# Moving the r, k and v projections of an RWKV-7 layer from its preparation into its loop over head pairs, and starting the network's first loads before a side calculation

## The chip, the cores and the metric

The kernel runs on one core of a Trainium2 chip. That core has TensorE (PE in the profile, with PEld for its weight loads), VectorE (DVE), ScalarE (ACT), GpSimd (POOL), and SyncE (SP), which here only issues DMAs. The metric is the time of one execution on the device in microseconds (us); lower is better.

## The reference

A network of four layers works on 512 tokens (256 of context, 256 noisy) of width 1024. The token mixer of layers 0 and 3 is a gated DeltaNet, of layer 1 an S5 state-space model, of layer 2 RWKV-7; a SwiGLU feed-forward follows each. Before each half a layer's input is normalised, scaled and shifted by numbers made from the conditioning vectors `c` and `c_ctx` ("modulation"). Layer 2, the one that is changed most, is cut here to what matters:

```python
dx = shifted - h
xr, xw, xk, xv, xa, xg = [h + dx * mu[j] for j in range(6)]
r = xr @ w_rkv[0]
k = xk @ w_rkv[1]
v = xv @ w_rkv[2]
g = jax.nn.sigmoid(xg @ g1) @ g2
kk = l2norm(heads(k * k_k))
for d in range(2):      # both directions
    logw = -jax.nn.softplus(-(w0[d] + jnp.tanh(xw @ w1[d]) @ w2[d])) - 0.5
    decay = jnp.exp(-jnp.exp(logw))
    a = jax.nn.sigmoid(a0[d] + (xa @ a1[d]) @ a2[d])
    k_d = k * (1.0 + (a - 1.0) * k_a)
...
def step(S, xs):        # one token, per head and direction, heads of 64
    sa = einsum('bhvk,bhk->bhv', S, kk_t)
    S = S * w_t - sa * (kk_t * a_t) + v_t * k_t
    return S, einsum('bhvk,bhk->bhv', S, r_t)
...
out = (groupnorm(y) * ln_w + ln_b + bonus) * g  @ w_out
```

## The kernel before

All activations lie with channels on the 128 partitions and the 512 tokens along the free axis, so a 1024-wide activation is eight tiles of 128x512. A dense product (`dense8`) is done in split precision: weights and activations are cut into a rounded half and its remainder (`whi`, `wlo`; `rhi`, `rlo`), ScalarE making the first and VectorE the second, and `mm3` issues three 512-column products (L135 to L137) for each 128x128 block of weights, 24 for an output tile. One such group of three is called a dense group below.

Instructions are issued to each engine in one fixed order, which a scheduler sets when the kernel is built. An instruction that waits holds up all that stand behind it in the order of its engine. For SP that order is also the order of nearly all DMAs.

**Outset.** `body` (L1719) first calls `net.s5_params()` (L674 to L738): a chain of small VectorE and ScalarE operations on the S5 parameters, which stores its outcome (`pk`) and loads it back (`s5pk`). Then it makes the modulation of layer 0 by `mods` (L169 to L183): 32 tiles `mraw` of 256 KB stream in and go through TensorE (L171). Then layer 0 begins with `norm`, which calls `rstd` (squares L194, sums L196, a product with ones L201), multiplies (L217), and splits for the first dense products.

**RWKV preparation** (`rwkv`, the part with the pool "rwa"). `mix(j)` makes one of the six mixed inputs: eight L1080 operations on VectorE, eight rounded halves on ScalarE (L158), eight remainders (L159), of which every second goes to GpSimd. `low` makes a low-rank input. `main` runs over the eight 128-channel tiles f, each a pair of heads: a dense product for r, k or v, copied and stored to HBM, and then one of the low-rank outputs (decay with its scan L1131, rate, gate), stored as well.

**Pair loop** (`RwkvCore`, the part with the pool "rwb"). For each pair: `load_in` reads k, r, the decays and rates back and forms exponentials and products; `gram` multiplies keys and queries chunk by chunk (64 tokens; L1527) into two masked tiles GK and GR; `invert` inverts the triangular 64x64 chunk matrices, whose 32-row diagonal blocks `fsub` inverts on VectorE alone, in 31 steps of two operations (L437, L439); `tokens` prepares what each chunk adds; `chain` walks over the 8 chunks in both directions at once (L1646 S to bank, L1656, L1662, L1668, L1670), each step needing the one before; `finish` normalises, gates and multiplies by the output weights into the residual X (dense groups with `yh`). While the chains of pair f run, `Lane` objects hand out the steps of other pairs' work between their steps, `n` steps spread over `over` chain steps, begun `lag` steps late: `finish` of f-1, `invert` and `tokens` of f+1, `load_in` and `gram` of f+2.

Of the kernel before, what the change touches and what calls it, by code (L numbers as in the profile page):

```python
# [12 lines left out]
F32 = mybir.dt.float32  # L13
# [6 lines left out]
P = 128  # L20
# [7 lines left out]
class Net:  # L28
    def __init__(self, tc, d, ctx):
# [11 lines left out]
        self.last_act = None  # L41
        cp = self.cp
# [163 lines left out]
    def norm(self, l, which, ts=slice(0, T), f32=None, f3=False):  # L206
# [7 lines left out]
        r = self.rstd(ts)  # L214
# [812 lines left out]
    def rwkv(self, l, nxt):  # L1027
# [4 lines left out]
        with ExitStack() as st:  # L1032
# [24 lines left out]
            rm = cn([P, T], "rmark")  # L1057
            G.memset(rm, 1.0)
            G.memset(rm[:, 0:T:64], 0.0)
            gneps = cn([P, 1], "gneps")  # L1060
            G.memset(gneps, 64e-5)
            par = self.fsub_marks(cpool)
            spill = lambda n: dp.tile([KD, P, T], F32, name=self.nm(n), tag=n)
            sp = {n: spill("rw_" + n) for n in ("r", "k", "v", "c0", "c1", "a0", "a1", "g")}

            with self.weights(), self.banks(w=4), tc.tile_pool(name="rwa", bufs=1, reuse_waits="tile") as ap:
                lora = [[ap.tile([P, T], F32R, name=self.nm("lo"), tag=f"lo{n}{x}") for x in range(2)]
# [7 lines left out]
                def mix(j):  # L1075
                    new = lambda n, k: ap.tile([P, T], F32R, name=self.nm(n), tag=f"{n}{k}", bufs=2)
                    hh = [], []
                    for k in range(KD):
                        t = self.tmp()
                        V.scalar_tensor_tensor(t, dx[k], mu(j, k), hf[k], op0=mul, op1=add)  # L1080
                        hh[0].append(new("rhi", k))
                        hh[1].append(new("rlo", k))
                        self.sub = G if k % 2 else V
                        self.split(t, hh[0][k], hh[1][k])
                    self.sub = V
# [24 lines left out]
                def main(n, hh, extra):  # L1110
                    self.hhi, self.hlo = hh
                    for f in range(KD):
                        ps = self.dense8(d["rwkv_rkv"]["rkv".index(n), f])
                        t, put = store(n, f)
                        A.copy(t, ps)
                        put()
# [35 lines left out]
                main("k", hk, ("rwkv_a2", rate))  # L1152
                low(2, hl)
                main("v", mix(3), ("rwkv_g2", gate))
# [4 lines left out]
            with self.weights(2), self.banks(c=2, o=1, w=2, g=1), \  # L1159
# [3 lines left out]
                for x in (core.load_in(0, st[0]), core.gram(0, st[0]), core.load_in(1, st[1]), core.invert(st[0]),  # L1163
                          core.tokens(0, st[0]), core.gram(1, st[1])):
# [3 lines left out]
                for f in range(KD):  # L1168
                    o = self.ps("o")
                    lanes = [Lane(late, 10, 28, 2)]  # L1170
                    if f < KD - 1:
                        n = st[f + 1]
                        lanes += [Lane(core.invert(n), 36, 34), Lane(core.tokens(f + 1, n), 11, 14)]
                    if f < KD - 2:
                        n = st[f + 2]
                        lanes += [Lane(core.load_in(f + 2, n), 6, 14), Lane(core.gram(f + 2, n), 13, 16, 16)]
# [273 lines left out]
class RwkvCore:  # L1450
# [15 lines left out]
    def load_in(self, f, out):  # L1466
# [5 lines left out]
        k, r = self.load("k", f), self.load("r", f, 1)  # L1472
        c, a = [[self.load(f"{n}{dr}", f) for dr in range(2)] for n in "ca"]
        out.update(r=r, a=a, kd=[], Pp=[], Pi=[])
# [11 lines left out]
        for dr in range(2):  # L1486
# [4 lines left out]
            G.tensor_tensor(kd, kd, k, op=mul)  # L1491
            G.tensor_tensor(a[dr], a[dr], kn, op=mul)
            for n, t in (("Pp", Pp), ("Pi", Pi), ("kd", kd)):
                out[n].append(t)
            yield

    def gram(self, f, out):
# [4 lines left out]
        D = new("fsD", [P, 16, 32], 2)  # L1502
# [5 lines left out]
        for dr in range(2):  # L1508
# [6 lines left out]
            G.tensor_tensor(q4(BK[:, :, 0:64]), n4(a), n4(Pi), op=mul)  # L1515
            V.tensor_tensor(q4(KR[:, :, 64:128]), n4(r), n4(Pp), op=mul)
            G.tensor_tensor(q4(BK[:, :, 64:128]), n4(kd), n4(Pi), op=mul)
# [4 lines left out]
            gk, gr = new("GK", [P, 2, 8, 64], 4), new("GR", [P, 2, 8, 64], 4)  # L1522
            for h in range(2):
                for c0 in (0, 4):
                    pg = net.ps("g").rearrange("p (c n) -> p c n", c=4)
                    for c in range(4):
                        mm(pg[:, c], BK[H[h], c0 + c, 64 * h:64 * h + 128], KR[H[h], c0 + c], start=True, stop=True)  # L1527
                    V.tensor_tensor(gk[:, h, c0:c0 + 4], pg[:, :, 0:64],
# [286 lines left out]
```

## Time and profile before

| | us |
|---|---|
| median of 3 runs (range) | 4115.85 (4113.26 to 4117.21) |
| the profiled execution's own time | 4122.03 |
| its span in the profile | 4120.3 |
| TensorE busy | 3692.1 (90%) |
| VectorE busy | 2596.9 (63%) |
| ScalarE busy | 1984.0 (48%) |
| GpSimd busy | 486.7 (12%) |
| HBM traffic by DMA | 432.71 MB, mean 105 GB/s |

The busy times are sums over the whole span, and the stages of the network have different limits, so they are only a first orientation. [...] The layer 2 mixer runs from about 1977 to 2857 us of the span.

### The profile page before, as it was taken

To read this page: it belongs to the slowest core of one execution; us is meant where nothing else is said; L and a number is where in the kernel's file an instruction comes from. 1 tells how busy PE (TensorE), PEld (TensorE's weight loads), DVE (VectorE), ACT (ScalarE), POOL (GpSimd) and SP (SyncE) were. 2 spreads that over 40 slices of the span, in tenths; PEclk is the share of its full clock that TensorE was granted. 3 is DMA by queue.
4 is the path that set the end of the run, shared out by engine and by line. 5 is a ranking of instruction groups with operands and counts; after the bars stand their busy time and mean duration, and the time that the engine had idled before them with its cause. 6 is when DMAs were issued, how large, how long until landed. Compare 5 with 4: busy or idle time off the path is not lost.

```text
span 4120.3 us, 75194 instructions
## 1 busy us (share of the span) xinstructions
PE 3692.1 (90%) x28906; PEld 2865.7 (70%) x28906; DVE 2596.9 (63%) x6045; ACT 1984.0 (48%) x4291; POOL 486.7 (12%) x625
## 2 busy tenths in 40 slices
PE   3889999989999798999795899997999978899899
PEld 1667777757777676777564666674777767787798
DVE  4777788767776743333874466665333487888665
ACT  4566677653333334232552333434322367778654
POOL 0000000012222200000212343430000000000000
PEclk8999999989999898999896566678999987999999
DMA  4312111135665623444342111001445311121155
GB/s 149 116 65 87 53 48 50 45 98 187 208 209 175 246 92 121 156 157 134 104 165 99 37 37 40 29 19 61 134 159 159 96 63 32 53 71 55 58 178 161
DMA packets 243624, 432.71 MB, mean 105 GB/s; under 512 B 27968, under 2 KB 53184, under 8 KB 240832
## 3 DMA queue, kind: packets, MB, share of 16 engines
q1 hardware_dynamic: 243264, 427.90, 32.0%
q8 instruction: 227, 3.72, 0.4%
q14 instruction: 133, 1.09, 0.1%
HBM read 383.49 MB, written 44.30 MB: 104 GB/s over the span
## 4 chain that ended last, share of the span: by engine, by line
PE 73%; DVE 12%; ACT 8%; DMA 3%; issue 2%; POOL 1%; SPq 0%; DVEq 0%; ACTq 0%; POOLq 0%
PE psd L135 10%; PE psd L136 10%; PE psd L137 9%; PE psw L135 7%; PE psw L136 7%; PE psw L137 7%; DMA mraw<-in_modw 2%; PE psm L171 2%; PE psg L1527 2%; PE psi L528 2%; PE pso L1670 1%; PE pso L1668 1%; PE psc L1381 1%; PE pso L1393 1%; DVE wlo L129 1%
## 5 line engine op out<-in xcount | busy, mean ns | idle before, releaser
L129 DVE TENSOR_TENSOR wlo<-wraw,whi 128x512 fp32r<-128x512 f32 (+1 forms) x906 | 622.6, 689 | 711.3 <-ACT whi L128 684.1
L128 ACT CAST whi<-wraw 128x512 fp32r<-128x512 f32 (+1 forms) x906 | 553.2, 613 | 1045.5 <-PE psd L136 591.8
L135 PE MATMUL psw<-hhi,whi 128*128 128x512 f32 (+1 forms) x1536 | 589.0, 383 | 26.7 <-ACT q L370 8.0
L137 PE MATMUL psw<-hhi,wlo 128*128 128x512 f32 (+1 forms) x1536 | 572.2, 373 | 0.1
L136 PE MATMUL psw<-hlo,whi 128*128 128x512 f32 (+1 forms) x1536 | 571.8, 372 | 0.4 <-DVE hlo L159 0.4
L135 PEld LDWEIGHTS psw<-hhi,whi 128*128 128x128 f32 x1536 | 296.4, 193 | 99.1 <-ACT whi L128 12.9
L137 PEld LDWEIGHTS psw<-hhi,wlo 128*128 128x128 f32 x1536 | 295.1, 192 | 51.6 <-issue 2.5
L136 PEld LDWEIGHTS psw<-hlo,whi 128*128 128x128 f32 x1536 | 296.3, 193 | 47.5 <-issue 3.1
L135 PE MATMUL psd<-hhi,whi 128*128 128x512 f32 (+1 forms) x784 | 296.0, 378 | 14.8 <-ACT hhi L158 14.8
L136 PE MATMUL psd<-hlo,whi 128*128 128x512 f32 (+1 forms) x784 | 289.6, 370 | 0.0
L137 PE MATMUL psd<-hhi,wlo 128*128 128x512 f32 (+1 forms) x784 | 288.9, 368 | 0.2 <-DVE wlo L129 0.2
L135 PE MATMUL psd<-fh,whi 128*128 128x512 f32 (+1 forms) x704 | 261.3, 371 | 0.0
L136 PE MATMUL psd<-fl,whi 128*128 128x512 f32 (+1 forms) x704 | 257.3, 366 | 0.0
L137 PE MATMUL psd<-fh,wlo 128*128 128x512 f32 (+1 forms) x704 | 256.8, 365 | 0.0
L237 DVE SCALAR_TENSOR_TENSOR X<-psd,modT,X 128x256 f32<-128x256 f32 x376 | 165.9, 479 | 110.3 <-PE psd L137 109.3
L171 PE MATMUL psm<-mraw,cs 128*32 128x256 f32 x1280 | 144.3, 416 | 68.5 <-DMA mraw<-in_modw 67.8
L135 PEld LDWEIGHTS psd<-hhi,whi 128*128 128x128 f32 x784 | 149.1, 190 | 62.6 <-ACT hhi L158 19.8
L136 PEld LDWEIGHTS psd<-hlo,whi 128*128 128x128 f32 x784 | 148.9, 190 | 28.0 <-DVE hlo L159 3.0
L137 PEld LDWEIGHTS psd<-hhi,wlo 128*128 128x128 f32 x784 | 149.2, 190 | 24.9 <-DVE wlo L129 0.6
L135 PEld LDWEIGHTS psd<-fh,whi 128*128 128x128 f32 x704 | 132.9, 189 | 34.5 <-ACT whi L128 11.1
L137 PEld LDWEIGHTS psd<-fh,wlo 128*128 128x128 f32 x704 | 133.0, 189 | 21.7
L136 PEld LDWEIGHTS psd<-fl,whi 128*128 128x128 f32 x704 | 133.0, 189 | 21.6 <-issue 1.6
(529 smaller groups left out, 7939.2 us busy)
## 6 DMA issues: line engine op xcount, KB each, us to landing
mraw<-in_modw SPq DMA_DIRECT2D x384, 256.0 KB, 3.3
wraw<-in_ffnin SPq DMA_DIRECT2D x352, 256.0 KB, 3.0
wraw<-in_gdn_qkvz SPq DMA_DIRECT2D x192, 256.0 KB, 2.7
wraw<-in_ffnout SPq DMA_DIRECT2D x160, 256.0 KB, 2.8
wraw<-in_gdn_out SPq DMA_DIRECT2D x64, 256.0 KB, 2.6
wraw<-in_rwkv_rkv SPq DMA_DIRECT2D x48, 256.0 KB, 3.0
s5ca<-ca SPq DMA_DIRECT2D x32, 256.0 KB, 3.1
s5in<-it SPq DMA_DIRECT2D x32, 256.0 KB, 4.2
```

Of the source, the lines that this page charges most:

```text
L128: nc.scalar.copy(hi[:, :n], raw[:, :n])
L129: self.sub.tensor_tensor(lo[:, :n], raw[:, :n], hi[:, :n].bitcast(F32), op=ALU.subtract)
L135: mm(out, whi, ahi, start=start, stop=False)
L136: mm(out, whi, alo, start=False, stop=False)
L137: mm(out, wlo, ahi, start=False, stop=stop)
L171: nc.tensor.matmul(ps[64 * x + 32 * q:64 * x + 32 * q + 32, :256], self.cs[:, k, :], w[:, q * 256:q * 256 + 256], start=(k == 0), stop=(k ...
L237: nc.vector.scalar_tensor_tensor(self.X[:, f, c], ps[:, c], self.modT[l][:, gate, f, s:s + 1], self.X[:, f, c], op0=ALU.mult, op1=ALU.add)
L528: mm(o, x, y, start=True, stop=True)
L1381: mm(p, Z[:, dr * 8 + v * 4 + c], x, start=True, stop=True)
L1393: mm(oc, w, at[hd][:, cs], start=first, stop=(step % 2 == 1 and hd == 3))
L1527: mm(pg[:, c], BK[H[h], c0 + c, 64 * h:64 * h + 128], KR[H[h], c0 + c], start=True, stop=True)
L1668: mm(o[H[h], cs], S[H[h]], KR[H[h], c, 64:128][:, rev], start=first[h], stop=False)
```

## The change

**Outset.** `body` begins the modulation first: seven steps of `mods`, then `net.rstd()`, whose result `norm` later takes from `net.early`, then `s5_params`, then the rest of `mods`.

**RWKV preparation.** `main` makes r, k and v only for the first two pairs; the halves of the three mixed inputs are stored to HBM instead (`rw_x`, 48 stores of 256 KB). All remainders are made on VectorE. `mix(3)` stands ahead of `low(2)`.

**Pair loop.** A new step `project` makes r, k and v of pair f+2 while pair f runs: for each of the three outputs, eight dense groups, each with its 512 KB of both halves (`vx`, three buffers) loaded anew, and weights in half tiles (`halves`), 144 such loads for six pairs. `load_in` of f+2 follows late in the same pair, and `gram` moves from f+2 to f+1. `gram` alternates the two heads and takes two banks of w at once; both its masks are now on VectorE, its copies on ScalarE. `invert` uses `sub16`, which inverts 16-row blocks in 14 steps of two VectorE operations and joins them with 128 small TensorE products (32x16). GpSimd's products and scalings go to VectorE and ScalarE. PSUM banks are shared out as c2, o1, w3 instead of c2, o1, w2, g1; the two banks `d` of dense products stay.

```diff
+        self.early = None
...
-        r = self.rstd(ts)
+        r = self.early or self.rstd(ts)
+        self.early = None
...
-                        self.sub = G if k % 2 else V
                         self.split(t, hh[0][k], hh[1][k])
-                    self.sub = V
...
                     self.hhi, self.hlo = hh
+                    j = "rkv".index(n)
+                    for k, parts in enumerate(zip(*hh)):
+                        for x in range(2):
+                            nc.sync.dma_start(sp["x"][j][k][:, x], parts[x].bitcast(F32))
                     for f in range(KD):
-                        ps = self.dense8(d["rwkv_rkv"]["rkv".index(n), f])
-                        t, put = store(n, f)
-                        A.copy(t, ps)
-                        put()
+                        if f < 2:
+                            ps = self.dense8(d["rwkv_rkv"][j, f])
+                            t, put = store(n, f)
+                            A.copy(t, ps)
+                            put()
...
-            with self.weights(2), self.banks(c=2, o=1, w=2, g=1), \
+            with self.weights(4), self.banks(c=2, o=1, w=3), \
...
-                for x in (core.load_in(0, st[0]), core.gram(0, st[0]), core.load_in(1, st[1]), core.invert(st[0]),
-                          core.tokens(0, st[0]), core.gram(1, st[1])):
+                for x in (core.fetch(0, st[0]), core.load_in(0, st[0]), core.gram(0, st[0]), core.invert(st[0]),
+                          core.tokens(0, st[0]), core.fetch(1, st[1]), core.load_in(1, st[1])):
...
-                    lanes = [Lane(late, 10, 28, 2)]
+                    lanes = [Lane(late, 12, 22, 2)]
                     if f < KD - 1:
                         n = st[f + 1]
-                        lanes += [Lane(core.invert(n), 36, 34), Lane(core.tokens(f + 1, n), 11, 14)]
+                        lanes += [Lane(core.gram(f + 1, n), 12, 12), Lane(core.invert(n), 22, 20, 13),
+                                  Lane(core.tokens(f + 1, n), 11, 16, 13)]
                     if f < KD - 2:
                         n = st[f + 2]
-                        lanes += [Lane(core.load_in(f + 2, n), 6, 14), Lane(core.gram(f + 2, n), 13, 16, 16)]
+                        lanes += [Lane(core.project(f + 2, n), 27, 31), Lane(core.load_in(f + 2, n), 6, 6, 28)]
...
+    def project(self, f, out):
+
+        net, nc, new = self.net, self.nc, self.new
+        for n in "krv":
+            j = "rkv".index(n)
+            ps = net.ps("d")
+            for k, w in enumerate(self.halves(net.d["rwkv_rkv"][j, f])):
+                x = new("vx", [P, 2, T], 3)
+                nc.sync.dma_start(x, self.sp["x"][j][k])
+                x = x.bitcast(F32R)
+                net.mm3(ps, *w, x[:, 0], x[:, 1], k == 0, k == KD - 1)
+                yield
+            t = out[n] = new("in_" + n)
+            nc.scalar.copy(t, ps)
             yield
...
+            for c0 in (0, 4):
+                pg = [net.ps("w").rearrange("p (c n) -> p c n", c=4) for _ in H]
+                for c in range(4):
+                    for h in range(2):
+                        mm(pg[h][:, c], BK[H[h], c0 + c, 64 * h:64 * h + 128], KR[H[h], c0 + c], start=True, stop=True)
...
-        TD = yield from net.fsub(self.gp, self.par, out["D"], lambda n: new(n, [P, 16, 32]))
+        TD, UD = yield from net.sub16(self.gp, self.par, D, lambda x, u: D[x, u],
...
-        w = net.wtile(net.d["rwkv_out"][f])
+        w = self.halves(net.d["rwkv_out"][f])
...
-                if 1 in layers:
-                    net.s5_params()
+                with tc.tile_pool(name="first", bufs=32, reuse_waits="tile") as fp, net.banks(m=2):
+                    first = net.mods(l, range(2 if l == 0 else 6), "m", net.raw_tile(fp, bufs=32))
+                    for _ in range(7):
+                        next(first)
+                    net.early = net.rstd()
+                    if 1 in layers:
+                        net.s5_params()
+                    for _ in first:
+                        pass
```

The first place is the order of DMAs on SP at the outset; `prm` and `s5pk` belong to `s5_params`, `mraw` to the modulation, `wraw` are weights of layer 0. Before:

```order
L71 DMA cc<-in_cc 128x16
L674 DMA prm_107<-in_s_prm 128x192
L738 DMA s5pk<-pk 128x2560
L169 DMA mraw_277<-in_modw 128x512
...
L169 DMA mraw_407<-in_modw 128x512
L1218 DMA cw_493<-in_gdn_conv 128x160
L1221 DMA gnw_496<-in_gdn_norm 128x1
L320 DMA dtb_595<-in_gdn_dtb 64x2
L127 DMA wraw_600<-in_gdn_ab 128x512
```

With the change:

```order
L72 DMA cc<-in_cc 128x16
L170 DMA mraw_105<-in_modw 128x512
...
L170 DMA mraw_157<-in_modw 128x512
L676 DMA prm_197<-in_s_prm 128x192
L170 DMA mraw_360<-in_modw 128x512
...
L170 DMA mraw_434<-in_modw 128x512
L128 DMA wraw_600<-in_gdn_ab 128x512
...
L128 DMA wraw_807<-in_gdn_qkvz 128x512
L740 DMA s5pk<-pk 128x2560
L128 DMA wraw_874<-in_gdn_qkvz 128x512
```

The modulation's loads now stand right behind the inputs, and `s5pk` has moved behind them and behind the first weights.

The second place is TensorE in the second half of a pair in the middle of the loop; L1646 and L1656 (L1692 and L1702 with the change) are the two products of the chain between which VectorE makes `x`. Before:

```order
L1646 MATMUL psc_21130<-S_24203,KR_22690 64x64 x2
L1668 MATMUL pso_23793<-KR_22690,S_24203 64x64
L1646 MATMUL psc_21131<-S_24247,KR_22814 64x64 x2
L1656 MATMUL psc_21130<-x_24241,U_23714 64x64 x2
L1656 MATMUL psc_21131<-x_24278,U_23714 64x64 x2
L1670 MATMUL pso_23793<-GR_22719,VS_23070 64x64
```

With the change (`vx` are streamed inputs of the projection, L507 is `sub16`):

```order
L1692 MATMUL psc_20475<-S_24480,KR_22914 64x64 x2
L1714 MATMUL pso_23905<-KR_22914,S_24480 64x64
L1692 MATMUL psc_20476<-S_24534,KR_23030 64x64 x2
L507 MATMUL psw_24706<-fsL_24223,fsUD_24614 32x16 x36
L1702 MATMUL psc_20475<-x_24528,U_23806 64x64 x2
L507 MATMUL psw_24706<-fsL_24223,fsUD_24614 32x16 x19
L136 MATMUL psd_24439<-vx_24771,whi_24470 128x512
L137 MATMUL psd_24439<-vx_24771,whi_24470 128x512
L138 MATMUL psd_24439<-vx_24771,wlo_24471 128x512
L136 MATMUL psd_24926<-vx_24933,whi_24928 128x512
L137 MATMUL psd_24926<-vx_24933,whi_24928 128x512
L138 MATMUL psd_24926<-vx_24933,wlo_24929 128x512
```

Between the steps of the chain now stand dense groups of the projection and the products of the new inverse.

The third place is TensorE at the end of a pair, where the Gram products (L1527, then L1575) stand. Before:

```order
L1527 MATMUL psg_24196<-KR_24166,BK_24167 128x128 x4
L1479 MATMUL psd_24628<-acc,bd_19087 128x512
L1702 MATMUL psd_24691<-t_24689,bdm_19088 128x512
L1527 MATMUL psg_24213<-KR_24166,BK_24167 128x128 x4
L1605 MATMUL psw_24451<-fsTD_24435,GK_23456 32x32 x16
```

With the change:

```order
L1716 MATMUL pso_23905<-GR_23056,VS_23435 64x64
L1742 MATMUL psd_24963<-t_24896,bdm_19088 128x512
L1575 MATMUL psw_24914<-KR_24900,BK_24901 128x128
L1575 MATMUL psw_24915<-KR_24900,BK_24901 128x128
L1575 MATMUL psw_24914<-KR_24900,BK_24901 128x128
L1575 MATMUL psw_24915<-KR_24900,BK_24901 128x128
...
L1575 MATMUL psw_24915<-KR_24900,BK_24901 128x128
L136 MATMUL psd_24926<-vx_25026,whi_24947 128x512
L137 MATMUL psd_24926<-vx_25026,whi_24947 128x512
L138 MATMUL psd_24926<-vx_25026,wlo_24948 128x512
L1702 MATMUL psc_20475<-XV_24413,U_24799 64x64
```

Runs of products into one bank became products that change bank and head at each instruction in the first half of the tokens, beside dense groups and the first step of the next pair's chain.

## Rows read from the trace of the kernel before

**Rows 1.** The page: granted TensorE clock in 40 slices of the span, tenths

```profile
PEclk8999999989999898999896566678999987999999
```

**Rows 2.** Windows: stretch; length; busy PE, PEld, DVE, ACT, POOL; clock; DMA share; GB/s

```profile
1977.00:2196.00 219.00, 182.05 (x769) 137.16 (x770) 156.59 (x252) 114.58 (x215) 43.24 (x28) 0.91 0.44 148
2196.00:2290.00 94.00, 36.48 (x287) 27.28 (x286) 46.17 (x106) 26.65 (x49) 32.25 (x32) 0.54 0.17 56
2290.00:2857.00 567.00, 529.24 (x4776) 383.46 (x4774) 348.68 (x1016) 206.59 (x560) 199.79 (x277) 0.70 0.11 32
```

**Rows 3.** SP timeline at the outset: start, duration, line, transfer, count

```profile
4.72 0.48 SPq L674 DMA_DIRECT2D prm<-in_s_prm  x1
32.38 0.33 SPq L738 DMA_DIRECT2D s5pk<-pk  x1
36.85 21.27 SPq L169 DMA_DIRECT2D mraw<-in_modw  x32
```

**Rows 4.** TensorE timeline at the outset, first dense product

```profile
79.70 0.79 PE L135 MATMUL psd<-hhi,whi 128*128 128x512 f32 x1 [4.78 <-ACT hhi L158]
```

**Rows 5.** VectorE groups, 1977 to 2196: count | busy us, mean ns | idle before

```profile
L1080 DVE SCALAR_TENSOR_TENSOR t<-dx,rprm,hf 128x512 f32<-128x512 f32 x48 | 46.4, 999 | 0.0
L129 DVE TENSOR_TENSOR wlo<-wraw,whi 128x512 fp32r<-128x512 f32 x54 | 39.8, 744 | 41.7 <-ACT whi L128 29.3 <-DMA wraw<-in_rwkv_rkv 2.8 <-DMA lw<-in_rwkv_g 2.0
L159 DVE TENSOR_TENSOR rlo<-t,rhi 128x512 fp32r<-128x512 f32 x24 | 22.8, 958 | 2.0 <-ACT rhi L158 2.0
```

**Rows 6.** A window of the RWKV preparation (columns as in the second group)

```profile
2040.00:2060.00 20.00, 20.00 (x92) 15.55 (x91) 19.00 (x30) 10.62 (x20) 0.00 (x0) 1.00 0.84 290
```

**Rows 7.** TensorE timeline between preparation and pair loop

```profile
2238.38 2.04 PE L1527 MATMUL psg<-KR,BK 64*128 64x128 f32 x8 [1.05 <-ACT GR L1530]
2241.34 2.07 PE L1527 MATMUL psg<-KR,BK 64*128 64x128 f32 x8 [0.92 <-ACT GR L1530]
...
2272.00 1.92 PE L1605 MATMUL psw<-fsTD,GK 32*32 32x32 f32 x64 [22.60 <-DVE fsTD L442]
```

**Rows 8.** VectorE group of the sub-block inverse in layer 0, 300 to 780

```profile
L483 DVE TENSOR_TENSOR fsL<-fsL,fsP 128x14 f32<-128x14 f32 (+6 forms) x70 | 13.8, 197 | 0.8
```

**Rows 9.** Windows inside the pair loop

```profile
2520.00:2541.00 21.00, 20.41 (x191) 15.59 (x185) 9.79 (x19) 7.53 (x19) 14.00 (x17) 0.54 0.11 33
2541.00:2562.00 21.00, 18.86 (x222) 13.90 (x221) 16.32 (x40) 8.59 (x23) 9.32 (x13) 0.98 0.26 76
```

**Rows 10.** A window inside the layer 0 loop

```profile
420.00:540.00 120.00, 111.66 (x1253) 90.06 (x1252) 94.38 (x231) 83.08 (x182) 3.05 (x6) 0.97 0.14 47
```

**Rows 11.** TensorE groups of 512-column products, layer 0 loop, 300 to 780

```profile
L135 PE MATMUL psw<-hhi,whi 128*128 128x512 f32 x243 | 101.5, 418 | 5.1 <-ACT t L370 2.9 <-ACT kT L370 2.1
L135 PE MATMUL psd<-Y,whi 128*128 128x512 f32 x95 | 41.3, 434 | 0.9 <-ACT whi L128 0.9
```

**Rows 12.** The TensorE group of the Gram products, pair loop

```profile
L1527 PE MATMUL psg<-KR,BK 64*128 64x128 f32 x434 | 92.2, 374 | 2.9 <-ACT GR L1530 2.3 <-DVE KR L1516 0.5
```

**Rows 13.** TensorE timeline at full clock, dense products among others

```profile
2548.20 0.51 PE L137 MATMUL psd<-yh,wlo 128*128 128x512 f32 x1
2548.55 0.39 PE L135 MATMUL psd<-yh,whi 128*128 128x512 f32 x1
...
2549.00 0.40 PE L137 MATMUL psd<-yh,wlo 128*128 128x512 f32 x1
2549.33 0.33 PE L1560 MATMUL psw<-ident,BK 64*128 64x64 f32 x2
```

**Rows 14.** TensorE timeline at full clock, Gram and chain products

```profile
2543.12 1.16 PE L1527 MATMUL psg<-KR,BK 64*128 64x128 f32 x8
2544.21 0.27 PE L1646 MATMUL psc<-S,KR 64*64 64x64 f32 x1
...
2827.36 0.33 PE L1646 MATMUL psc<-S,KR 64*64 64x64 f32 x4
2827.61 0.74 PE L1656 MATMUL psc<-x,U 64*64 64x64 f32 x8
```

## Prediction on record

> **What bounds the kernel now.** I read the granted clock by slices first, then windows by stage, then in each stage the timeline and the groups of the engine that the others wait for. The clock by slices shows one long dip [rows 1], and the windows place it: it is the RWKV mixer's second half. Three stretches matter [rows 2]. In the preparation (1977 to 2196, 219 us) TensorE is busy for 182 us and VectorE for 157, so both are nearly full. Between it and the first chain step (94 us) TensorE is busy for 36: there the stretch is a string of dependent steps. In the pair loop (567 us for eight pairs, 71 each) TensorE is busy for 529 at a mean clock of 0.70; VectorE has 349, ScalarE 207 and GpSimd 200, all far from full. The loop is bound by TensorE, and by TensorE running slow. Its clock is not even: 21 us at 0.54 stand right beside 21 us at 0.98 [rows 9]. The layer 0 loop holds 0.97 with TensorE busy for 112 of 120 us [rows 10].
>
> At the outset SP stands at `s5pk` until `s5_params` is through (32.38), and the 32 modulation tiles begin only when that has landed, at 36.85 [rows 3]; the first dense product starts at 79.70 [rows 4].
>
> The sum is made against the profiled execution's 4122.0 us; the median is 6.2 lower.
>
> **Outset.** The 32 loads took 21.3 us to issue [rows 3]; the first can now issue where `prm` did, at 4.7 [rows 3]. Estimate: 4.7 + 21.3, and about 6 more because the 2 MB of X are in flight at the same time (at the same 8.4 MB in 21.3 us), so they are in by 32. In the trace 79.7 - (36.85 + 21.27) = 21.6 us lay between the last issue and the first dense product, and squares, sums and the product with ones, some 10 us of it, now stand ahead. So the first dense product comes at 32 + 11 = 43, 37 earlier. The side calculation's VectorE operations now run among those of the norm; if these must wait for all of it the gain falls to some 30, and without the X term it is 43. I take **-38**.
>
> **Preparation.** It loses 18 x 24 = 432 dense products. At 0.23 us each [rows 13] that is 98 of TensorE's 182 us, which leaves 84. VectorE then sets the pace: of its 157 us it loses 36 `wlo` at 0.744 (27 us) and gains 24 remainders from GpSimd; with a partner on GpSimd L1080 takes 0.999 and `rlo` 0.958, where the same size took 0.744 in `wlo` [rows 5]. At 0.744 for all the sum is 157 - 27 + 18 - 12 - 5 = 131, at 0.958 for the new ones and nothing else it is 153. With VectorE full at 131 the stretch gains 88, at 153 filled to nine tenths 49. I take **-60**. The 48 new stores (12.6 MB) find room: the busiest window moved 290 GB/s [rows 6] where the stretch averages 148 [rows 2].
>
> **Between.** The Gram tiles of pair 0 follow each other every 2.96 us, each waiting for ScalarE to empty the one bank [rows 7]. Eight of them at the product's own 2.07 would save 7 us. The inverse made TensorE wait 22.6 us for `fsub` [rows 7]; 28 operations of 0.197 [rows 8] make 5.5 us, I put 15 to 16 for them with gaps, transposes and the two joins through TensorE, so 7 us less. GpSimd's part goes to a faster engine and pair 1's Gram leaves: 8 us in all. Against it 72 dense products of pair 2 are now queued here, ahead of the inverse's: 17 us at full clock, 33 at half, in 58 idle us. Their 24 loads of 512 KB need 43 us at 290 GB/s [rows 6], so they fit too, but not by much. From -35 (all hidden) to +10 (half of them exposed and the other savings halved); I take **-25**.
>
> **Loop.** Its work in microseconds of full clock is 567 x 0.70 = 397. To it come
> - 360 dense products (432 less the 72) at 0.23: +83;
> - what it costs to put them among other shapes. The last product ahead of a run starts 0.35 before the next one, and 0.33 pass after its last [rows 13], where inside the run it is 0.23: 0.1 at each end. For 120 groups in twos that is 60 x 0.2 = +12 (0 if hidden, 24 alone);
> - the 128 small products and their joins for 7 pairs: 64 of such a size took 1.92 us at the low clock [rows 7], so about 2 us a pair at full: +14;
> - the Gram products: 8 take 1.09 us, while 4 chain products that change heads take 0.25 [rows 14]. These are half as wide, so by the column nothing is gained to, at most, half of 434 x 0.136 = 59 us [rows 12]; the row of the same width is nearer: -10 of a possible -30.
>
> Sum 397 + 83 + 12 + 14 - 10 = 496. [...]
>
> The clock decides what becomes of 496. In the layer 0 loop 3 x 338 dense products stand in 480 us [rows 11], 0.23 x 1014 / 480 = 48% of the time, at 0.97 [rows 10]. Here it is 192 products (64 groups of `finish`), 8% of the time, at 0.70. With the change it would be 552 products in some 590 us, 22%. On the straight line between the two the clock is 0.79; since a group now stands in nearly every chain step, while before they came in one run per pair (the 0.98 window, with its weights' 76 GB/s [rows 9], is such a run), I take 0.84: 496 / 0.84 = 590, **+23**. Bounds: 0.97 gives 511 (-56), 0.70 gives 709 (+142).
>
> VectorE in the loop: 349 / 8 = 44 us a pair [rows 2], less some 12 for the inverse, plus 7 from GpSimd, 3 for masks, 5 for weights: 47 of some 74, hidden. If it were not, a pair could not fall under 47. ScalarE rises from 26 to some 36, hidden likewise.
>
> **Sum.** -38 - 60 - 25 + 23 = -100: 4022 for the profiled execution, **4016** by the median.
>
> **Rivals.**
> - *The clock rises to the layer 0 loop's level.* For it: the 0.98 window. Against it: only 22% dense. Loop 511, total 4016 - 79 = 3937.
> - *The clock does not rise.* For it: rows at 0.54 with TensorE busy for 20.4 of 21 us [rows 9], so busy time alone does not bring it. Loop 709, total 4016 + 119 = 4135, slower than before. It decides from a loop of about 690, a clock of 0.72. A pair would take 100 us and TensorE would be full throughout.
> - *The streamed inputs come late.* A group that waits for its `vx` holds up the chain's products behind it. With three buffers a load can be issued three groups ahead, some 9 us where groups stand one per chain step, but 4 to 5 where they stand in twos, as in the order; 512 KB at 290 GB/s are 1.8 us plus the landing. I expect no wait. If each of the 120 waits 0.5 us, it is +60: 4076; at 0.8 all gain is gone.
> - *The preparation does not follow VectorE* but the string ScalarE, VectorE, TensorE at each mixed input: half the gain, 4046.
> - *The one bank left to `wout`*, while a projection holds the other, makes 64 groups wait about 0.5 us for the residual on VectorE, with chain products behind them: +30 at most, in the same range.
>
> **Chances.** My forecast (clock 0.77 to 0.92, between 3970 and 4070, the two small rivals included): 0.52. Clock at 0.92 or above, under 3970: 0.22. Late inputs, or a clock of 0.72 to 0.77, 4070 to 4108: 0.09. Clock not rising, or late inputs above 0.8 us: 0.17, of which 0.04 lie within 0.2% of before. Two tenths of a per cent (8 us) is about what a measurement of this kernel can tell from no change. For 8 in 10 the range runs from 3935 to 4100. Faster 0.83, same 0.04, slower 0.13.
>
> **What would show it.** Outset: the first `mraw` issue at about 5 and the first dense product near 43. Preparation: VectorE nearly full, the stretch near 160. Between: about 70. Loop: a clock of 0.8 or more in its windows, TensorE busy for over nine tenths, pairs of 70 to 77 us for the first six, and the chain of waits still on TensorE. It is wrong if TensorE's idle time in the loop ends on `vx` loads, or if the clock stays near 0.7, or if VectorE ends the waits there.

## The result and the profile after

The changed kernel takes 4019.78 us, the median of 4 runs (4012.52 to 4024.64); the kernel before took 4116.53 beside it. The ratio is 0.9763, with a 95% interval of 0.9743 to 0.9782: 2.4% faster, 97 us, where the prediction on record had 100. The profiled execution took 4024.64 by its own time, 97 less than that of before (4122.03). Three disturbed executions, two of the kernel before (7565 and 5793) and one of run e5 (4557), are left out of the ratios.

On the page (first the busy sums, then the granted clock by slices, in tenths of the full, as in [rows 1]) the sum of TensorE's busy time is almost the same as before, and the long dip of the clock is shorter and shallower:

```profile
PE 3677.6 (91%) x30954; PEld 2827.6 (70%) x30954; DVE 2558.7 (64%) x5962; ACT 2039.2 (51%) x4421; POOL 225.8 (6%) x312
...
PEclk8999999989999898999787899868999888999899
```

The windows of the RWKV mixer after the change answer to [rows 2]: preparation, what lies between, pair loop (length, busy PE, PEld, DVE, ACT, POOL, clock, DMA share, GB/s):

```profile
1934.00:2076.00 142.00, 100.13 (x340) 62.54 (x338) 123.71 (x244) 87.49 (x165) 2.45 (x4) 0.79 0.64 224
2076.00:2149.00 73.00, 46.04 (x580) 32.82 (x580) 36.79 (x92) 29.59 (x54) 0.00 (x0) 0.64 0.62 210
2149.00:2755.00 606.00, 587.91 (x6958) 415.87 (x6956) 348.41 (x954) 288.31 (x738) 6.23 (x12) 0.85 0.44 145
```

The preparation went from 219 to 142 us, the part between from 94 to 73. The loop grew from 567 to 606, with a clock of 0.85 in the place of 0.70, and 145 GB/s in the place of 32.

At the outset, SP and the first dense product on TensorE, beside [rows 3, 4]:

```profile
4.46 11.25 SPq L170 DMA_DIRECT2D mraw<-in_modw  x14
...
50.92 0.33 SPq L740 DMA_DIRECT2D s5pk<-pk  x1
```

```profile
42.59 0.79 PE L136 MATMUL psd<-hhi,whi 128*128 128x512 f32 x1 [5.61 <-ACT hhi L159]
```

The modulation's first load issues at 4.46, `s5pk` waits until 50.92 behind all that is urgent, and the first dense product starts 37.1 us earlier than at 79.70.

The stages add up for the two profiled executions. In the table the stages run from one TensorE instruction to another: first dense product, the RWKV norm's product with ones, last low-rank product, first chain step, the feed-forward norm's product with ones (so the edges lie a few us beside those of the windows).

| stage | before | after | change |
|---|---|---|---|
| to the first dense product | 79.7 | 42.6 | -37.1 |
| to the RWKV norm | 1899.5 | 1894.2 | -5.3 |
| RWKV preparation | 217.2 | 139.0 | -78.2 |
| between | 93.9 | 73.5 | -20.4 |
| pair loop to the next norm | 570.4 | 609.7 | +39.3 |
| the rest | 1259.6 | 1263.9 | +4.3 |
| span | 4120.3 | 4022.9 | -97.4 |

The pair loop's two rows (columns as above), before and after:

```profile
2290.34:2860.69 570.35, 528.96 (x4773) 383.27 (x4771) 352.22 (x1022) 209.57 (x564) 199.79 (x277) 0.70 0.11 32
```

```profile
2149.31:2759.01 609.70, 587.99 (x6958) 415.90 (x6957) 352.27 (x961) 290.99 (x742) 6.23 (x12) 0.85 0.44 144
```

Below, length times granted clock is called the us of full clock that a stretch holds: 570.4 x 0.70 = 399 before, 609.7 x 0.85 = 518 after.

In the preparation VectorE's two large groups show why it shrank more than was said (count, busy, mean ns; compare [rows 5]): all 48 mixes now take 0.744 each and all 48 remainders 0.684.

```profile
L1083 DVE SCALAR_TENSOR_TENSOR t<-dx,rprm,hf 128x512 f32<-128x512 f32 x48 | 34.7, 744 | 0.0
L160 DVE TENSOR_TENSOR rlo<-t,rhi 128x512 fp32r<-128x512 f32 x48 | 31.8, 684 | 0.7 <-ACT rhi L159 0.7
```

In the part between, TensorE's waits (us in total, times, longest) show the streamed inputs, 7.0 us, but more for the string of small steps of `load_in`:

```profile
PE psd L1488 <- ACT acc L1485: 14.3, 2, 8.3
PE psd L136 <- DMA vx<-rw_x: 7.0, 8, 1.5
```

In the loop the inputs cost 1.9 us in all. TensorE is idle for 18 of the 606 us, and these are its longest waits:

```profile
PE psd L136 <- ACT yh L159: 4.7, 2, 4.4
PE pso L1716 <- ACT VS L1704: 3.1, 7, 1.4
PE psd L136 <- DVE X L239: 2.0, 4, 0.9
PE psd L136 <- DMA vx<-rw_x: 1.9, 4, 1.0
```

And the clock of the pairs: one in the middle of the loop, with a projection beside it, and the last two, which have none:

```profile
2387.75:2460.37 72.62, 71.92 (x961) 51.27 (x961) 47.81 (x132) 40.56 (x102) 1.04 (x2) 1.00 0.67 222
2618.42:2689.80 71.38, 68.26 (x872) 49.99 (x871) 33.26 (x102) 30.04 (x82) 0.00 (x0) 0.69 0.03 9
2689.80:2759.01 69.21, 55.13 (x352) 34.73 (x351) 32.59 (x79) 23.85 (x64) 0.00 (x0) 0.70 0.10 31
```

### The profile page after: what moved, and what is told of

It reads as the page before. It is cut to its first block, busy times and chain, and to the rows that moved or that the text cites. A ratio compares the mean times of both kernels' runs of the same rounds, so it can differ in the third digit from the quotient of the medians.

```text
span 4022.9 us, 79144 instructions
## 1 busy us (share of the span) xinstructions
PE 3677.6 (91%) x30954; PEld 2827.6 (70%) x30954; DVE 2558.7 (64%) x5962; ACT 2039.2 (51%) x4421; POOL 225.8 (6%) x312
## 4 chain that ended last, share of the span: by engine, by line
PE 75%; DVE 10%; ACT 9%; DMA 3%; issue 2%; SPq 0%; POOL 0%; DVEq 0%; ACTq 0%
PE psd L136 11%; PE psd L137 10%; PE psd L138 10%; PE psw L136 8%; PE psw L137 7%; PE psw L138 7%; PE psm L172 2%; DMA mraw<-in_modw 2%; PE psi L530 2%; PE pso L1716 1%; PE pso L1714 1%; PE psw L1575 1%; PE psc L1390 1%; PE pso L1402 1%; DMA vx<-rw_x 1%
## 5 line engine op out<-in xcount | busy, mean ns | idle before, releaser
L129 ACT CAST whi<-wraw 128x512 fp32r<-128x512 f32 x854 | 521.3, 613 | 975.9 <-PE psd L137 548.3
L130 DVE TENSOR_TENSOR wlo<-wraw,whi 128x512 fp32r<-128x512 f32 x854 | 582.9, 685 | 653.6 <-ACT whi L129 645.7
```

Source lines behind the costliest of these rows:

```text
L129: nc.scalar.copy(hi[:, :n], raw[:, :n])
L130: self.sub.tensor_tensor(lo[:, :n], raw[:, :n], hi[:, :n].bitcast(F32), op=ALU.subtract)
```

## Experiments

"Loop" and "preparation" below are the stages of the table, from each run's profile. The times are medians, with the ratio to the kernel before.

### The outset alone (e1_outset)

The kernel before with `early`, and `body` as in the diff ahead of the prediction.

> The kernel before with the outset's change alone. In the trace of the changed kernel the first dense product came 37 us earlier, and the stretch from there to the RWKV preparation was 6 us shorter. If both belong to the outset, this kernel takes 4116 - 43 = 4073 us; if only the first dense product does, 4079; if an earlier start is given back later (weights and modulation loads that now meet), 4090 or more.

Measured: 4104.84, ratio 0.9962 (0.9947 to 0.9977): 12 us faster, not 37 or more. The profile has the gain where it was expected: first dense product at 42.2, RWKV norm at 1938.2, 41 us ahead of before. Then it is lost in a loop whose code was not touched. Its windows (whole loop, then two neighbouring pairs):

```profile
2249.36:2856.70 607.34, 563.38 (x4772) 408.74 (x4770) 356.15 (x1022) 210.83 (x564) 200.23 (x277) 0.65 0.10 30
2411.84:2511.00 99.16, 92.40 (x677) 66.91 (x676) 55.73 (x154) 30.82 (x81) 34.55 (x46) 0.62 0.09 28
2511.00:2576.62 65.62, 62.60 (x589) 45.54 (x589) 43.24 (x127) 25.25 (x69) 24.59 (x33) 0.63 0.13 42
```

607 us at 0.65 against 570 at 0.70: in us of full clock 395 against 399, so the loop holds the same work and takes longer by its clock. This profiled execution, at 4121, is the slowest of the six that were timed (4097 to 4121), and its mean clock over the whole span is 0.899, where the one at 4097 has 0.907. Of the three expectations the third, a gain given back, holds by its number; but the place is the loop, at a lower clock, and not loads that meet. Instructions in the loop do stand in another order here, since the scheduler laid out the whole program anew. The order is the same in all six executions, so it does not make the 24 us between them; whether it makes the loss of the median is not shown.

### The RWKV part alone (e9_rwkv_part_alone) and useless products beside the outset (e10_idle_products_and_outset)

The first is the changed kernel with the old outset in `body` and `norm`. The second adds the outset to the kernel e6 below.

> The changed kernel with the outset of before: the change's second half alone. The outset alone gave 12 us where its first dense product came 37 us earlier and the RWKV preparation began 41 us earlier; the loop of that kernel took 607 us at a clock of 0.65 where that of before took 570 at 0.70. If the two halves of the change simply add up, this kernel takes 4020 + 12 = 4032. If the outset's 41 us are earned in full where the loop's clock does not fall (theory), it takes 4020 + 41 = 4061, with a loop near 606 as in the changed kernel.

> The kernel before with the 16 useless dense groups a pair and with the outset of the changed kernel. Theory (the outset alone lost its gain to the loop's clock, which dense products hold up): the loop stays near 588 at 0.83, and the whole is 4140 less 41: 4099. If the loss has another cause (loads that meet, a different order), 4140 less 12: 4128.

Measured: e9 4051.77, ratio 0.9851 (0.9828 to 0.9875). Beside a loop at 0.86 the outset is worth 4051.8 - 4019.8 = 32 us, nearer to its 41 than to the 12 it gave alone; the two halves alone give 12 and 64 us, together 97. e10: 4105.30, ratio 0.9973 (0.9957 to 0.9989), 34 us less than e6 without the outset, and the same as e1's 4104.84: beside the new outset the useless products cost nothing. Both lie between the two expectations and nearer to the theory's. The loops of the two profiled executions:

```profile
2181.60:2788.70 607.10, 584.04 (x6958) 414.60 (x6957) 353.07 (x961) 290.61 (x741) 6.21 (x12) 0.86 0.44 145
```

```profile
2247.50:2855.40 607.90, 580.50 (x5103) 411.39 (x5101) 346.96 (x1022) 209.77 (x564) 196.51 (x277) 0.80 0.10 30
```

So the new outset brings the first dense product 36 to 38 us earlier in each kernel (42.2 and 43.3 here, 79.7 and 78.8 without it), and less of that is given back where dense products stand in the loop: 34 and 32 us are left, against 12 in e1. Why the loop gives it back is not shown. e10's profiled run, at 4119.9, is the slowest of ten (4094 to 4120), with its loop at 0.80 instead of e6's 0.83: also there something is given back.

### All of r, k and v in the preparation (e2_all_in_preparation)

```diff
-                    for k, parts in enumerate(zip(*hh)):
-                        for x in range(2):
-                            nc.sync.dma_start(sp["x"][j][k][:, x], parts[x].bitcast(F32))
...
-                        if f < 2:
+                        if f < KD:
...
-                        lanes += [Lane(core.project(f + 2, n), 27, 31), Lane(core.load_in(f + 2, n), 6, 6, 28)]
+                        lanes += [Lane(core.fetch(f + 2, n), 1, 4), Lane(core.load_in(f + 2, n), 6, 6, 28)]
```

> The changed kernel, but with r, k and v of all pairs made in the preparation as before and fetched in the loop: no streamed inputs, no dense products of the projection between the chains. Theory (the projection's products raise the clock of the loop): the preparation grows by about 65 us, the loop loses 384 products of 0.23 us (88 at full clock, of 515), but its clock falls back from 0.85 to about 0.70, so it takes 427 / 0.70 = 610 and gains nothing; the whole is about 4085. Rival (the clock of 0.85 comes from the alternating Gram products and the new inverse): 427 / 0.85 = 502 in the loop, the whole 4020 + 65 - 104 = 3981.

Measured: 4044.39, ratio 0.9818 (0.9798 to 0.9838): 25 us slower than the changed kernel. Preparation and loop:

```profile
1933.90:2135.40 201.50, 179.03 (x770) 135.74 (x770) 143.98 (x268) 112.94 (x213) 2.08 (x4) 0.93 0.48 158
2202.90:2780.40 577.50, 550.14 (x6574) 402.34 (x6573) 330.85 (x929) 264.10 (x691) 6.21 (x12) 0.67 0.10 31
```

The preparation grows by 62.5 us, the part between falls by 6.0, and the loop falls by 32.2 only, from 609.7 to 577.5, though 384 dense products have left it: its clock is 0.67 again. In us of full clock that loop holds 577.5 x 0.67 = 387, the changed one 609.7 x 0.85 = 518. The move put 131 us of full clock into the loop for 32 us of time. The theory's clock came, but its 610 us and 4085 did not: it put the work that is left at 427 instead of 387. The rival (clock 0.85 without the projections, 3981) is out. This loop has 1800 products more than that of the kernel before (6574 against 4773), all of them small, and its clock is no higher (0.67 against 0.70): more instructions alone do not raise it.

### Useless products in the kernel before (e6_idle_products_before) and in the last pairs (e5_idle_products_last_pairs)

```diff
+    def fill(self, n):
+        net, nc, x = self.net, self.nc, self.fx
+        for _ in range(n):
+            ps = net.ps("d")
+            for i in range(3):
+                nc.tensor.matmul(ps, x[:, :P], x, start=i == 0, stop=i == 2)
+            yield
...
+                    lanes += [Lane(core.fill(16), 16, 31)]
```

In e5, on the changed kernel, it is `fill(12)` for the last two pairs, with `x` from one loaded `vx`.

> The kernel before with useless work added: 16 dense groups in every pair of the loop (384 products of 512 columns, about as many as the changed kernel's projections have there; nothing is streamed, results not used). Theory (dense products raise the clock): 397 us of full clock plus 88 and some 12 for the change of shapes, at about 0.85 as in the changed kernel: 585 instead of 567, the whole some 4130, with the loop's clock at 0.82 or more. Rival (the clock does not follow them): 497 / 0.70 = 710, the whole some 4255.

> The changed kernel with useless work added: in the last two pairs, which have no projection, 12 dense groups each (72 products of 512 columns in all, on data that is loaded once, results not used). In the changed kernel these pairs take 71 and 69 us at a clock of 0.69 and 0.70, where pairs with a projection have 0.82 to 1.00. Theory (dense products between the chain's steps raise the clock): their work of 49 us of full clock each becomes 57, at 0.85 to 0.95 that is 60 to 67 us a pair, so the kernel gets faster by 6 to 15 us although it does more: about 4010. Rival (the clock there has another cause): 16 us of work more at 0.70, +24: 4044.

Measured: e6 4139.74, ratio 1.0062 (1.0043 to 1.0081). 384 products, 88 us at full clock, cost 24 us. Of them 54 stand ahead of the loop's first chain step, where TensorE was idle for much of the time; 330 (76 us) stand in the loop:

```profile
2287.00:2875.00 588.00, 560.99 (x5102) 399.04 (x5101) 348.64 (x1022) 209.98 (x564) 195.83 (x277) 0.83 0.11 31
```

0.83 in the place of 0.70, 588 us, 18 more than before; the theory said 585 and at least 0.82, the rival 710. Nothing else of the change is in this kernel, so dense products raise the clock by themselves.

e5: its three executions take 4018 to 4025, ratio 0.9771 (0.9751 to 0.9791), the same as the changed kernel's 0.9763: between theory (4010) and rival (4044). The last two pairs:

```profile
2618.91:2688.72 69.81, 69.81 (x906) 50.90 (x904) 34.40 (x105) 28.59 (x79) 0.00 (x0) 0.84 0.03 9
2688.72:2757.57 68.85, 56.01 (x386) 35.45 (x386) 32.53 (x80) 24.61 (x65) 0.00 (x0) 0.85 0.09 31
```

Their clock is 0.84 and 0.85 where it was 0.69 and 0.70, and they take 69.8 and 68.9 us where they took 71.4 and 69.2. 16 us of added work were free, but did not pay as the theory had it (60 to 67 us a pair). TensorE waits for nothing in the first of the two (busy for 69.8 of 69.8), so the room that the clock gives is just used up.

### The Gram products head by head (e3_gram_head_by_head)

```diff
-                for c in range(4):
-                    for h in range(2):
+                for h in range(2):
+                    for c in range(4):
```

> The changed kernel with the Gram products of one head after those of the other, all else (two banks at once, masks, copies) the same. The rows of the changed kernel give 24 alternating products in 2.2 us, 0.091 each, where before they stood 0.136 apart: 0.045 x 448 = 20 us of full clock, at 0.85 some 24 us: 4044. By the value that the prediction took (10 at full clock) it is 4032. If weight loads were hidden already, 4020.

Measured: 4044.49, ratio 0.9807 (0.9782 to 0.9832), the 24 us that were expected; but the trace does not bear out the reason. In both kernels a run of 24 Gram products stands ahead of a dense group between preparation and loop, first in the changed kernel, then here:

```profile
2104.71 2.26 PE L1575 MATMUL psw<-KR,BK 64*128 64x128 f32 x24
2106.90 0.50 PE L136 MATMUL psd<-vx,whi 128*128 128x512 f32 x1
```

```profile
2102.69 2.42 PE L1575 MATMUL psw<-KR,BK 64*128 64x128 f32 x24
2105.04 0.51 PE L136 MATMUL psd<-vx,whi 128*128 128x512 f32 x1
```

2.19 us against 2.35: 0.091 and 0.098 a product. The second run began at a lower clock: the dense products just ahead of it start 0.42 to 0.43 us apart (2101.28, 2101.71, 2102.13), those behind it 0.23 to 0.34. So heads that alternate save at most 0.007 x 448 = 3 us of full clock, not 20; summed over the loop, from start to start at the granted clock, these products take 47 and 48 us. The 0.136 that I had read from [rows 14] came from a run of eight with the change of shape at its end in it (inside it they stand 0.112 apart, at its end 0.20), which the longer runs over two banks spread; what else makes these faster is not separated. So the 4044 was met by luck. What the loop lost lies mainly in one pair, at a low clock:

```profile
2147.60:2782.40 634.80, 607.74 (x6957) 433.26 (x6957) 353.66 (x961) 291.28 (x742) 6.22 (x12) 0.83 0.42 138
2457.48:2562.01 104.53, 102.50 (x985) 72.22 (x984) 52.23 (x141) 44.13 (x107) 1.09 (x3) 0.70 0.45 151
```

104.5 us at 0.70, the pairs on either side 74 to 76. Its five executions lie from 4020 to 4049, with a mean clock of 0.937 in the one and 0.925 in the other, so the loss comes in some and not in others, in one and the same order of instructions. What decides it stays open.

### Remainders back on GpSimd (e4_remainders_on_gpsimd)

```diff
+                        self.sub = G if k % 2 else V
                         self.split(t, hh[0][k], hh[1][k])
+                    self.sub = V
```

> The changed kernel with every second remainder of the mixed inputs back on GpSimd. Theory (VectorE sets the pace of the preparation, and is slowed while GpSimd works beside it): 24 remainders of 0.68 leave VectorE (-16 us), but 48 mixes go from 0.744 back to about 1.0 (+12) and the 24 others from 0.68 to 0.96 (+7): VectorE's sum is the same within 5 us, and the time with it, 4020 to 4027. Rival (VectorE is simply relieved): 4004.

Measured: 4038.63, ratio 0.9807 (0.9794 to 0.9821), 19 us slower: both expectations missed, in the direction of the theory. VectorE's groups in the preparation:

```profile
L1083 DVE SCALAR_TENSOR_TENSOR t<-dx,rprm,hf 128x512 f32<-128x512 f32 x48 | 44.7, 953 | 0.0
L160 DVE TENSOR_TENSOR rlo<-t,rhi 128x512 fp32r<-128x512 f32 x24 | 23.5, 983 | 1.4 <-ACT rhi L159 1.4
```

The mixes went from 0.744 to 0.953, the remainders that VectorE kept from 0.684 to 0.983, those of the weights from 0.685 to 0.917. Its scans (L1138, here L1140) did not slow: 1.217 and 1.211; in the kernel before, where they take 1.215, none of the 16 has a GpSimd operation beside it. VectorE does 24 operations less and is busy for 132.6 us instead of 121.4. The preparation takes 151.5 us instead of 139.0. The trace of the kernel before shows the same by operation: the 28 mixes that run with nothing on GpSimd beside them take 0.742 each, the 20 others 1.36; of the remainders, the 6 alone 0.682, the 18 others 1.05. What the two engines share is not shown.

### The old inverse in the loop (e8_fsub_in_the_loop)

`first` is set for pair 0 alone.

```diff
-        TD, UD = yield from net.sub16(self.gp, self.par, D, lambda x, u: D[x, u],
+        if not first:
+            TD = yield from net.fsub(self.gp, self.par, D, lambda n: new("fs", [P, 16, 32], 3))
+            UD = new("fs", [P, 16, 32], 3)
+            nc.vector.transpose(UD, TD)
+        else:
+            TD, UD = yield from net.sub16(self.gp, self.par, D, lambda x, u: D[x, u],
...
-                        lanes += [Lane(core.gram(f + 1, n), 12, 12), Lane(core.invert(n), 22, 20, 13),
+                        lanes += [Lane(core.gram(f + 1, n), 12, 12), Lane(core.invert(n), 36, 20, 13),
```

> The changed kernel with the old inverse for pairs 1 to 7, in the loop, and the new one only for pair 0, ahead of it. Theory (the loop is bound by TensorE, the new inverse's products are cost there): 256 small products a pair leave, 17 us of full clock in all, 20 at 0.85: 4000. Rival (VectorE, with 12 us a pair more, 62 steps that stand among the chain's, makes the chain wait): no gain, or 10 to 20 us more, with TensorE waiting for VectorE's x and S.

Measured: 4010.10, ratio 0.9750 (0.9724 to 0.9776). That is 10 us below the changed kernel, but the intervals overlap. The loop:

```profile
2150.10:2753.70 603.60, 563.19 (x5166) 398.43 (x5165) 402.66 (x1179) 282.12 (x725) 9.39 (x18) 0.84 0.43 145
```

It takes 603.6 us instead of 609.7, with VectorE busy for 403 instead of 352 and 603.6 x 0.84 = 507 us of full clock instead of 518, 11 less. Both expectations hold in part: TensorE is busy for 25 us less (563 instead of 588), as the theory had it, but idle for 40 instead of 22, as the rival had it. This profiled execution, at 4022, is the slowest of the four (3999 to 4022), so the 10 us of the medians are not all in these rows.

### Modulation in the last pairs (e7_modulation_last_pairs, e11_half_modulation_and_fsub)

```diff
+                mod = Lane(self.mods(l + 1, range(6), "d", lambda: core.new("vx", [P, 2, T], 3)[:, 0]), 48, 62)
...
-                        for x in lanes:
+                        for x in lanes + [mod] * (f >= KD - 2):
...
-            net.ffn(l, ts, l + 1 if l + 1 in layers else None)
+            net.ffn(l, ts, l + 1 if l + 1 in layers and l != 2 else None)
```

e11 is e8 with `range(3)` of it, the other three parts left in the feed-forward.

> The changed kernel with the modulation of layer 3 moved from layer 2's feed-forward into the last two pairs: useful work in the place of the useless work of the other run. Its 192 products of 256 columns (about 35 us busy at full clock) leave the feed-forward, which is bound by TensorE, and gives back some 30 us. Theory: the clock of the two pairs rises to about 0.85, they take 76 us instead of 70 each: the whole about 4000. Rival (these products, with 32 columns of weights, do not raise the clock): the pairs take 95 us each, the whole about 4040.

> The changed kernel with the old inverse for pairs 1 to 7 and with half of layer 3's modulation (three of six parts) in the last two pairs, the rest in the feed-forward as before. The old inverse in the loop gave 10 us, all six parts there 7 (the last pair then took 103 us, with TensorE idle for 21; the feed-forward and what follows 45 less). With half, the last pairs should take 75 and 70 us, 7 to 13 more than with the old inverse alone, and the rest 22 less: 4010 less 9 to 15: about 3998. If the half costs as much as it saves, 4010.

Measured: e7 4013.39, ratio 0.9768 (0.9743 to 0.9792); e11 4011.24, ratio 0.9741 (0.9719 to 0.9763), no better than e8. In e7 what follows the loop takes 1218 us instead of 1264, 45 less; but the last two pairs take 15 and 34 more than in the changed kernel:

```profile
2621.95:2708.35 86.40, 81.67 (x1058) 46.86 (x1056) 35.86 (x109) 30.42 (x83) 0.00 (x0) 0.90 0.47 145
2708.35:2811.72 103.37, 81.83 (x530) 39.51 (x529) 33.58 (x84) 23.81 (x64) 0.00 (x0) 0.75 0.37 117
```

So the clock did rise, as the theory had it, but the pairs did not take the 76 us that it gave them; the whole, 4013, lies between theory (4000) and rival (4040). In the second pair TensorE is idle for a fifth, 8.3 us of it until a load of modulation weights lands. That profiled execution took 4031.8, the other three 4012.6 to 4013.4. In e11 the loop takes 634.6 us, 31 more than in e8, for the 23 saved behind it; this profiled execution, at 4030, is the slowest of six (3999 to 4030):

```profile
2149.70:2784.30 634.60, 595.36 (x5364) 405.67 (x5363) 405.04 (x1185) 282.01 (x725) 9.40 (x18) 0.84 0.47 158
```

So none of these beats the changed kernel by more than the measurement can tell; e8 and e11 come nearest.

## Why the prediction was right, point by point

- **What bounds.** Right: the loop is bound by TensorE's clock. TensorE is idle for 18 of 606 us in it, and the loop's clock moves with the dense products that stand in it: 0.67 without the projection's and 0.85 with them (e2), 0.83 with useless ones in the kernel before and 0.70 without (e6), 0.84 and 0.85 in the last two pairs and 0.69 and 0.70 without (e5).
- **Outset, -38.** -37.1 in the profile, the first dense product at 42.6 where 43 was said; it is worth 32 us of the whole beside the RWKV part (e9). That the same 37 us give only 12 where the loop is the old one (e1) was not foreseen.
- **Preparation, -60.** -78.2. The step was right, the term mis-sized: VectorE's sum went to the lower of the two given (131 us) and below it, 121, because without GpSimd beside it the mixes and remainders are faster (0.744 and 0.684, where before they took 0.999 and 0.958), which e4 shows from the other side. Of the 78, e2 gives 62.5 to the products of r, k and v that left, and e4 12.5 to the remainders.
- **Between, -25.** -20.4. The three savings listed for it, 7 + 7 + 8, make 22, not the 35 of its lower end, so -25 left no room for the products of pair 2. In e2, where none are queued here, the part takes 67.5: the savings were 26, and the products cost 6.0 of them; TensorE waits for their inputs for 7.0 us.
- **Loop, +23.** +39.3, by a clock of 0.85 (0.84 was said) and work of 518 us of full clock (496). The 0.84 was picked above a straight line of 0.79 because a group stands in nearly every chain step; no run tests that reason, and with 330 such products e6 has 0.83 and e10 0.80. Two terms were too small, as sums over the loop's trace show (from the start of each product on TensorE to the start of the next, at the granted clock). The projection's products take 112 us; 83 + 12 was said. There are 384 and not 360 of them in the loop, since 48 and not 72 stand ahead of it; and the 12 held for groups in twos, while 64 of the 112 runs of these products are one group alone, at 0.90 us instead of 0.69:

```profile
2420.03 0.50 PE L136 MATMUL psd<-vx,whi 128*128 128x512 f32 x1
2420.37 0.39 PE L137 MATMUL psd<-vx,whi 128*128 128x512 f32 x1
2420.60 0.40 PE L138 MATMUL psd<-vx,wlo 128*128 128x512 f32 x1
2420.93 0.33 PE L1716 MATMUL pso<-GR,VS 128*64 128x64 f32 x2
```

The new inverse's products take 25; 14 was said. The trace counts each of these products twice: the 64 of [rows 7] are the 32 that `invert` issues there, so that the new 128 of a pair are 256 in the trace, and the price read from [rows 7] gives some 27. For the Gram products -10 was said, and they take 47 us instead of 57; but alternation itself gives 3 at most (e3), and which of the other changes gives the rest no run separates. All else in the loop takes 7 us less, for which nothing was said.

- **Sum.** Two errors of the same size, 18 too little gained in the preparation and 16 too little lost in the loop, cancelled. That 97 us came so near to 100 is luck; that the loop gets longer and the whole faster by some 2% is not. Taken back one at a time, the move of the projections is worth 25 us (e2), the outset 32 (e9), the remainders 19 (e4); since the loop's clock has a share in each, they need not add up.
- **Rivals.** The clock that does not rise is out; by e2, e5 and e6 it is the dense products that raise it. The clock of the layer 0 loop was reached in single pairs (1.00 above), not on the mean. Late inputs cost 1.9 us in the loop, and the waits for X, by which the one bank left to `wout` would show, 2.0 us. The preparation followed VectorE, which is busy for 121 of its 139 us: 11 us more of VectorE made it 12.5 longer (e4). The possible 30 of the Gram products, half of 434 x 0.136, was an estimate from [rows 12, 14]; the rows of e3 show 3 at most for alternation.

Still open: why the mean clock of the span differs between executions of the same program (0.899 to 0.907 in e1, 0.925 to 0.937 in e3, 0.925 to 0.934 in e10), which makes 24, 30 and 26 us; and what it is in the dense products (their width, or that they come in between) that raises the clock.

## What to carry to other kernels

Where a stretch of small products runs at a low clock (0.70 here), its room cannot be read from TensorE's busy time: 529 of 570 us were busy, and yet 330 wide products more, 76 us at full clock, made it only 18 us longer (e6). Before moving work, compare time times granted clock of the two places, and try wide products where the clock is low. This is no rule for all work: the modulation's products, which are 256 columns wide and wait for their loads, gained nothing there (e7, e11). And a gain ahead of such a stretch is only banked when the stretch's own time is looked at again.

## What the runs showed that I had not expected

- Useless work is nearly free there: 88 us of full clock for 24 (e6) and, beside the new outset, for nothing (e10 against e1); 16 us for nothing (e5).
- 37 us saved 1900 us earlier came out as 12 (e1), with a lower clock in a loop whose code was not changed.
- Taking 24 operations from VectorE made it busy for 11 us more (e4).
